# A hybrid decoder trunk on one core: VectorE, ScalarE and TensorE tied to the source's order up to the first up projection

## The chip, the core and the metric

The kernel runs on one core of a Trainium2 chip. A core has TensorE (PE in the rows of the profile, with PEld for its weight loads), VectorE (DVE), ScalarE (ACT), GpSimd (POOL) and SyncE (SP), each with a queue of instructions of its own, and DMA queues that bring data from HBM. The metric is the device time of one execution in microseconds (us).

## The reference

256 tokens of width 2048 go through two layers. Layer 0 mixes by sliding-window attention with grouped heads, layer 1 by a gated linear recurrence (HGRN2); each is followed by a squared-ReLU MLP of width 8192. Shift, scale and gate of every half layer come from a conditioning vector `c`.

```python
cond = jax.nn.silu(c)
for i in range(DEPTH):
    mod = cond @ mod_w[i] + mod_b[i]
    sh1, sc1, g1, sh2, sc2, g2 = jnp.split(mod, N_MOD, axis=-1)
    h = modulate(rms_norm(x, norm_mix[i]), sh1, sc1)
    ...
    x = x + g1[:, None, :] * y
    h = modulate(rms_norm(x, norm_mlp[i]), sh2, sc2)
    x = x + g2[:, None, :] * squared_relu_mlp(h, mlp_w1[i], mlp_w2[i])
```

In the attention `q` and `k` (32 query heads of 64, 4 key heads) are RMS-normed by head, the logits get a distance penalty (ALiBi) and a window of 128 keys, and the softmax has one more term, a learned sink per head.

## The kernel before

**Tiling.** Activations are kept transposed, 16 blocks of 128 features by 256 tokens (`x0` to `x3` hold four blocks each). Products are formed in fp32r with two parts: an operand `h` or `o` holds a high part (256 columns) and a low part (256 columns). A weight tile `raw` of 128 x 2048 comes by one DMA of 1 MB into one of 5 buffers; `prep_one` (L220) makes of each half `wh` (cast on ACT, L237) and `wl` (difference on DVE, L238). `three` (L353) issues the three matmuls of a step over a block: `wh` by the high part, `wh` by the low part, `wl` by the high part. 16 blocks, so 48 matmuls, use up one weight tile.

**What is prepared.** `prep_one` walks a list `seq` in which three kinds stand: weights; modulation rows that DVE multiplies with `cond` and sums (L226, tile `mods`); and modulation rows by a matrix-vector product on PE (`gemv`, L245): 16 matmuls `mm<-raw`, ACT's copy of the row `w<-mm` (L254), four transposes `gt` on PE, DVE's sum into `mods` (L260). `ahead` keeps it one or two weights ahead of the matmuls. `norm_first` (L468) and `norm_rstd` (L488) make the RMS norm, with a chain of small operations on `nsm`; `make_h` (L530) builds one block of the modulated input: `ht` on DVE (L534), the high part on ACT (L538), the low part on DVE (L539).

**Stages.** QKV runs over the first half of the blocks, then over two quarters, each time for ten columns (in a quarter one weight tile holds two). Within the last quarter `evac_k` (L642) and `evac_q` (L674) take a column up: a sum on DVE, a square on ACT, the matmuls `ssq` and `sst`, a chain for the reciprocal root (`head_rstd`, L617). From its third weight on, `step` (L780) is called three times behind each weight, and then until 16 steps are done. A step n issues the background queue (`hook`, L311), the product of probabilities and values of pair n-4 (`pair_v`, L751: matmuls `pv`, eight instructions in the trace, ACT's cast and DVE's low part of `o`), the transposes of pair n-3 (`pair_t`, L740: per head three transposes into the one buffer `pt`, ACT's copy `PT`), pair n itself (`pair`, L693) and up to two items of `seq` that are no weights. `pair` takes two heads: `S0` and `S1` on PE; scaling with the penalty and maximum on DVE (L707, L710); the maximum with the sink (L717 to L719); the exponentials with their sums on ACT (L720, L724); sum and reciprocal on DVE (L727, L728); and the probabilities, scaled half on ACT (L733), half on DVE (L736). Then come the out-projection and `open_mlp` (L837): residual columns between eight half products of the raw `x` (`mm_uhalf`, whose column sums go to `sums`, L877), the blocks h8 to h15 (L884 to L888), and eight rounds over the second half of the blocks (L890 to L904), in each of which a column is evacuated (L900, then the squared ReLU), one weight is read and one more block is built. The rest of the MLP and layer 1 follow.

**What sets the order.** The kernel is written once in source order; a scheduler then orders each engine's queue by the dependences, and may move an instruction ahead of others on its engine. Class `Queue` (L40) wraps an engine; where `pin` is set, each instruction gets a dependence without a semaphore on the one that this wrapper's list `last` holds, so that it can't be moved ahead of it. Before, `pep` is such a wrapper (the transposes and attention products), `pe` shares its list but isn't pinned, and DVE and ACT are used bare:

```python
dve, act, sp, pool_q = nc.vector, nc.scalar, nc.sync, nc.gpsimd
last = []
pe, pep = Queue(tc, nc.tensor, last, False), Queue(tc, nc.tensor, last, True)
```

Of the kernel before, what the change touches and what calls it, by code (L numbers as in the profile page):

```python
# [39 lines left out]
class Queue:  # L40


    def __init__(self, tc, engine, last, pin):
        self.tc, self.engine, self.last, self.pin = tc, engine, last, pin

    def __getattr__(self, name):
        fn = getattr(self.engine, name)

        def call(*args, **kw):
            r = fn(*args, **kw)  # L50
            if self.pin and self.last:
                self.tc.add_manual_dep(
                    r.ins, self.last[-1],
                    mybir.DependencyInfo(mybir.DependencyClass.NoSync, mybir.DependencyReason.DATA),
                    reason="issue order")
            self.last[:] = [r.ins.name]
            return r
        return call
# [2 lines left out]
@with_exitstack  # L61
def trunk(ctx, tc, a, out):
    nc = tc.nc
    dve, act, sp, pool_q = nc.vector, nc.scalar, nc.sync, nc.gpsimd
    last = []
    pe, pep = Queue(tc, nc.tensor, last, False), Queue(tc, nc.tensor, last, True)

# [198 lines left out]
    def prep_mods(l, which, upto=KB):  # L266
        while any((l, which * 16 + k) not in ready for k in range(upto)):
            if any(e[0] == "m" and e[1:] == (l, which * 16 + k) or e[0] == "g" and e[1] == l
                   and 0 <= which * 16 + k - e[2] < 4
                   for k in range(upto) for e in seq[st["prep"]:]):  # L270
                prep_one()
            else:
                hook()
# [32 lines left out]
    def later(delay, fn):  # L306
        bg.append((bgst["slot"] + delay, bgst["n"], fn))
        bgst["n"] += 1
        bg.sort(key=lambda e: (e[0], e[1]))
# [169 lines left out]
    def norm_add(kb):  # L479
        if kb == 0:  # L480
            nstate["ss"] = tmp.tile([P, T], F32, tag="rbs", name="ssum", bufs=1)
            act.activation(out=nstate["ss"], in_=X[kb], func=AF.Square)
            return
        sq = wt()
        act.activation(out=sq, in_=X[kb], func=AF.Square)
        dve.tensor_tensor(out=nstate["ss"], in0=nstate["ss"], in1=sq, op=ALU.add)

    def norm_rstd(sumcol=ones[:, :1]):  # L488
        ss = psum.tile([P, 2], F32, tag="sm", name="sst", bufs=1)
        for b in range(2):  # L490
            pe.matmul(ss[:, b:b + 1], lhsT=nstate["ss"][:, b * P:(b + 1) * P], rhs=sumcol,
                      start=True, stop=True)
        sm = tmp.tile([P, 8], F32, tag="nsm", name="nsm")
        dve.tensor_scalar(out=sm[:, 0:2], in0=ss, scalar1=1.0 / D, scalar2=EPS,
                          op0=ALU.mult, op1=ALU.add)
        rsqrt(sm[:, 0:2], sm[:, 2:4], sm[:, 4:6], sm[:, 6:8])
        dg = tmp.tile([P, T], F32, tag="dg", name="dg", bufs=1)
        for b in range(2):
            dve.tensor_scalar(out=dg[:, b * P:(b + 1) * P], in0=ident, scalar1=sm[:, 2 + b:3 + b],
                              scalar2=None, op0=ALU.mult)  # L500
        nstate["dg"] = dg

    def norm_bcast():
        rb = psum.tile([P, T], F32, tag="sm", name="rb", bufs=1)
        pe.matmul(rb, lhsT=ones, rhs=nstate["dg"], start=True, stop=True)
        rbs = tmp.tile([P, T], F32, tag="rbs", name="rbs", bufs=1)
        act.copy(out=rbs, in_=rb)
        return rbs
# [12 lines left out]
    def mod_prep(l, half, k0=0, n=KB):  # L521
        sh, sc = (SH1, SC1) if half == 0 else (SH2, SC2)
        mod_bias(l, sh, k0, n)
        mod_bias(l, sc, k0, n)
        g = l * 2 + half
        dve.scalar_tensor_tensor(out=gsc[:, g, k0:k0 + n],
                                 in0=mods[:, l, sc * 16 + k0: sc * 16 + k0 + n], scalar=1.0,
                                 in1=gains[:, g, k0:k0 + n], op0=ALU.add, op1=ALU.mult)

    def make_h(l, half, rbs, kb, s):  # L530
        sh = SH1 if half == 0 else SH2
        g = l * 2 + half
        t = tmp.tile([P, T], F32, tag="ht", name="ht", bufs=2)
        dve.scalar_tensor_tensor(out=t, in0=X[kb], scalar=gsc[:, g, kb:kb + 1], in1=rbs,  # L534
                                 op0=ALU.mult, op1=ALU.mult)
        shc = mods[:, l, sh * 16 + kb: sh * 16 + kb + 1]
        h = optile(sets[s], kb)
        act.activation(out=h[:, :T], in_=t, func=AF.Identity, bias=shc)  # L538
        dve.scalar_tensor_tensor(out=h[:, T:2 * T], in0=t, scalar=shc, in1=h[:, :T].bitcast(F32),  # L539
                                 op0=ALU.add, op1=ALU.subtract)  # L540
        return h
# [15 lines left out]
    def start_u(l, half, n=KB):  # L557
        sh = SH1 if half == 0 else SH2
        c = mods[:, l, sh * 16: sh * 16 + n]
        sw = tmp.tile([P, KB, 2], F32R, tag="sw", name="swt", bufs=1)  # L560
        act.copy(out=sw[:, :n, 0], in_=c)
        dve.tensor_tensor(out=sw[:, :n, 1], in0=c, in1=sw[:, :n, 0].bitcast(F32), op=ALU.subtract)
        ustate["sw"] = sw
        ustate["next"], ustate["lim"] = (l, half), n
        ustate["U"] = [None] * KB
# [5 lines left out]
    def evac_res(l, which, n):  # L571
        def f(ps):
            resid(l, which, n, ps)
            finish_x(n)
        return f
# [3 lines left out]
    def finish_x(n):  # L579
        if ustate["next"] is not None and n < ustate["lim"]:  # L580
            ustate["U"][n] = make_u(*ustate["next"], n)
        if n < KB - 1:
            later(2, lambda: norm_add(n))
        elif ustate["next"] is None:
            norm_add(n)
# [251 lines left out]
    def open_mlp(mp, A, relu2):  # L837
        prep_mods(0, SC2, KH)
        prep_mods(0, SH2, KH)
        mod_prep(0, 1, 0, KH)  # L840
        start_u(0, 1, KH)
        U = ustate["U"]
        for n in range(2):
            finish_x(n)
        parts, H, box = [], [None] * KB, {}
        sums = mp.tile([P, KB], F32, tag="sums", name="sums")

        def more_h(k0, k1):
            for k in range(k0, k1):
                H[k] = make_h(0, 1, box["rbs"], k, 0)  # L850

        def s2():
            box["rbs"] = norm_bcast()

        def s1():
            norm_rstd()
            later(NB, s2)

        def s0():
            norm_add(KB - 1)  # L860
            later(1, s1)

        def res(n):
            mm_std(O, evac_res(0, G1, n), fold=True)
            if n == KB - 1:
                later(1, s0)

        for kind, n in order[2:]:
            if kind == "o":
                res(n)  # L870
                continue
            part = mp.tile([P, 2 * T], F32, tag=f"acc{n}", name=f"part{n}")
            parts.append(part)

            def keep(u, ps):
                c = 2 * n + u
                dve.tensor_reduce(out=sums[:, c:c + 1], in_=ps[:, T:T + 2], axis=AX.X, op=ALU.add)  # L877
                act.copy(out=part[:, u * T:(u + 1) * T], in_=ps[:, :T])
            mm_uhalf(U, keep)
        while "rbs" not in box:  # L880
            hook()
        ustate["next"], ustate["lim"] = None, KB
        sets.reverse()
        for k in range(KH, KB, 2):  # L884
            prep_mods(0, SC2, k + 2)
            prep_mods(0, SH2, k + 2)
            mod_prep(0, 1, k, 2)
            more_h(k, k + 2)  # L888
        ahead(LAG - 1)
        for p in range(8):  # L890
            t2 = wt(2 * T)
            dve.tensor_tensor(out=t2.rearrange("p (a b) -> p a b", b=T),
                              in0=parts[p].rearrange("p (a b) -> p a b", b=T),
                              in1=box["rbs"].unsqueeze(1).to_broadcast([P, 2, T]), op=ALU.mult)

            def ev(ps):
                for u in range(2):
                    t = t2[:, u * T:(u + 1) * T]
                    n = 2 * p + u
                    dve.scalar_tensor_tensor(out=t, in0=ps[:, u * T:(u + 1) * T], scalar=sums[:, n:n + 1],  # L900
                                             in1=t, op0=ALU.add, op1=ALU.add)
                    relu2(A, n, t)
            mm_half(H, 1, ev)
            more_h(p, p + 1)  # L904
        return H

    def mlp_layer(l, H, last):
# [399 lines left out]
```

## Time and profile before

| what | value |
|---|---|
| runs | 2334.56, 2332.07, 2333.48 us |
| median | 2333.48 us |
| profiled execution | 2334.28 us |
| its span | 2332.5 us (1.8 us lie around it) |
| granted TensorE clock, mean | 0.987 |

A row of the profile's groups reads: line, engine, operation, out<-in (shapes), count, then busy time, mean in ns of one, and idle time before them with what ended it. A row of the timeline: start, duration, engine, line, operation, out<-in, count, and in brackets the idle time before it and its releaser. The windows give busy time and count of instructions of each engine in a stretch, the granted clock (PEclk, 1 is full), the DMA engines' busy share and GB/s.

### The profile page before, as it was taken

How to read it: one execution, taken by the hardware profiler on the slowest of the kernel's cores; microseconds unless marked ns; L12 is line 12 of the kernel's file. 1: busy time of each engine (PE TensorE's matmuls, PEld its weight loads, DVE VectorE, ACT ScalarE, POOL GpSimd, SP SyncE). 2: the span in 40 equal slices, each digit the busy share in tenths (PEclk: the TensorE clock that was granted, in tenths of full speed). 3: DMA queues.
4: the chain of work that ended last, by engine and by line, in shares of the span. 5: the costliest groups of instructions: out<-in, count | busy, mean ns of one | idle time of the engine just before them, and what ended most of it. 6: DMA issues, size and time to landing. Idle time of an engine off the chain costs nothing.

```text
span 2332.5 us, 36840 instructions
## 1 busy us (share of the span) xinstructions
PE 2263.7 (97%) x14538; PEld 1986.2 (85%) x14538; DVE 1818.7 (78%) x3061; ACT 1166.8 (50%) x1974; POOL 3.5 (0%) x10
## 2 busy tenths in 40 slices
PE   2989999999999999999999999999999999999999
PEld 0986489998888888888888988899888888888888
DVE  8888788966988988887998988767866766655665
ACT  2435754544444444455666666655544444444443
POOL 0000000000000000000000000000000000000000
PEclk6999999999999999999999999999999999999999
DMA  9987789556989889885577777545666666555552
GB/s 379 344 311 287 295 319 365 200 183 244 341 319 340 319 326 334 322 304 181 210 280 267 257 271 266 201 166 181 226 244 219 249 231 229 209 182 194 184 197 93
DMA packets 84637, 598.79 MB, mean 257 GB/s; under 512 B 9456, under 2 KB 11504, under 8 KB 12272
## 3 DMA queue, kind: packets, MB, share of 16 engines
q1 hardware_dynamic: 81936, 593.81, 70.7%
q8 instruction: 114, 1.87, 0.3%
q10 hardware_dynamic: 2304, 2.10, 0.3%
q0 software_dynamic: 224, 0.52, 0.1%
q14 instruction: 59, 0.48, 0.1%
HBM read 594.04 MB, written 2.10 MB: 256 GB/s over the span
## 4 chain that ended last, share of the span: by engine, by line
PE 94%; DVE 4%; DMA 1%; ACT 1%; issue 1%; ACTq 0%; DVEq 0%
PE mm L50 89%; DVE raw L226 2%; DVE wl L238 1%; PE S L50 1%; PE A L50 1%; PE pv L50 1%; PE pt L50 1%; DMA raw<-in_mod_w_dram 1%; PE on L50 0%; PE cb L50 0%; ACT wh L237 0%; PE ss L50 0%; DVE ht L534 0%; PE ssq L50 0%; PE sst L50 0%
## 5 line engine op out<-in xcount | busy, mean ns | idle before, releaser
L237 ACT CAST wh<-raw 128x1024 fp32r<-128x1024 f32 x744 | 779.3, 1051 | 892.3 <-PE mm L50 801.8
L238 DVE TENSOR_TENSOR wl<-raw,wh 128x1024 fp32r<-128x1024 f32 x744 | 907.3, 1223 | 401.7 <-ACT wh L237 399.3
L50 PE MATMUL mm<-h,wh 128*128 128x512 f32 (+2 forms) x3728 | 1152.6, 368 | 37.3 <-ACT wh L237 37.3
L50 PE MATMUL mm<-h,wl 128*128 128x256 f32 (+1 forms) x3232 | 907.2, 281 | 7.5 <-DVE wl L238 7.5
L50 PE MATMUL mm<-o,wh 128*128 128x512 f32 (+2 forms) x3120 | 859.1, 345 | 0.0
L50 PEld LDWEIGHTS mm<-h,wh 128*128 128x128 f32 x3728 | 672.2, 190 | 162.0 <-ACT wh L237 38.3
L50 PE MATMUL mm<-o,wl 128*128 128x256 f32 (+1 forms) x2432 | 679.5, 280 | 0.0
L50 PEld LDWEIGHTS mm<-h,wl 128*128 128x128 f32 x3232 | 612.4, 190 | 9.5 <-DVE wl L238 8.4
L50 PEld LDWEIGHTS mm<-o,wh 128*128 128x128 f32 x3120 | 538.3, 188 | 81.5 <-issue 1.3
L50 PEld LDWEIGHTS mm<-o,wl 128*128 128x128 f32 x2432 | 458.3, 189 | 0.4
L226 DVE CUSTOM_DVE_ANT_0 raw<-raw,cond 128x2048 f32<-128x2048 f32 x164 | 374.4, 2286 | 15.6 <-DMA raw<-in_mod_w_dram 11.5
L50 PE MATMUL mm<-wh,h 128*128 128x256 f32 x576 | 106.5, 284 | 4.2 <-DVE h L539 2.7
L50 PEld LDWEIGHTS mm<-wh,h 128*128 128x128 f32 x576 | 89.8, 190 | 5.3 <-DVE h L539 3.2
L50 PE MATMUL mm<-wl,h 128*128 128x256 f32 x288 | 81.5, 283 | 0.0
L459 ACT COPY w<-mm 128x256 f32<-128x256 f32 x186 | 67.7, 364 | 0.0
L463 ACT CAST h<-w 128x256 fp32r<-128x256 f32 x125 | 49.9, 404 | 25.6 <-DVE w L919 25.0
L50 PEld LDWEIGHTS mm<-wl,h 128*128 128x128 f32 x288 | 54.7, 190 | 0.6 <-issue 0.4
L919 DVE SCALAR_TENSOR_TENSOR w<-w 128x256 f32<-128x256 f32 x125 | 52.1, 423 | 2.2
L464 DVE TENSOR_TENSOR h<-w,h 128x256 fp32r<-128x256 f32 x125 | 51.7, 419 | 0.0
L460 DVE TENSOR_TENSOR w<-mm,w 128x256 f32<-128x256 f32 x109 | 45.6, 418 | 0.4 <-ACT w L459 0.2
L940 DVE TENSOR_TENSOR acc<-mm,acc 128x256 f32<-128x256 f32 x96 | 40.6, 423 | 6.2 <-PE mm L50 3.7
L939 DVE TENSOR_TENSOR acc<-acc,w 128x256 f32<-128x256 f32 x94 | 39.4, 419 | 7.1 <-ACT w L938 7.0
(200 smaller groups left out, 1098.4 us busy)
## 6 DMA issues: line engine op xcount, KB each, us to landing
raw<-in_mod_w_dram SPq DMA_DIRECT2D x164, 1024.0 KB, 5.7
raw<-in_mlp_dram SPq DMA_DIRECT2D x128, 1024.0 KB, 4.9
raw<-in_hin_dram SPq DMA_DIRECT2D x64, 1024.0 KB, 4.9
raw<-in_mlp1b_dram SPq DMA_DIRECT2D x64, 1024.0 KB, 4.9
raw<-in_mlp1a_dram SPq DMA_DIRECT2D x48, 1024.0 KB, 5.8
raw<-in_mod_g_dram SPq DMA_DIRECT2D x28, 1024.0 KB, 6.6
raw<-in_aout_dram SPq DMA_DIRECT2D x16, 1024.0 KB, 7.0
raw<-in_m1h_dram SPq DMA_DIRECT2D x16, 1024.0 KB, 6.6
```

The source lines that it names most:

```text
L50: r = fn(*args, **kw)
L226: dve.tensor_tensor_reduce(out=r, in0=r, in1=cond, scale=1.0, scalar=0.0, op0=ALU.mult, op1=ALU.add, accum_out=mods[:, e[1], e[2]:e[2] + 1])
L237: act.copy(out=wh, in_=part)
L238: dve.tensor_tensor(out=wl, in0=part, in1=wh.bitcast(F32), op=ALU.subtract)
L459: act.copy(out=t, in_=ps[:, T:])
L460: dve.tensor_tensor(out=out_t, in0=ps[:, :T], in1=t, op=ALU.add)
L463: act.copy(out=opt[:, :T], in_=src_t)
L464: dve.tensor_tensor(out=opt[:, T:2 * T], in0=src_t, in1=opt[:, :T].bitcast(F32), op=ALU.subtract)
L919: dve.scalar_tensor_tensor(out=t, in0=t, scalar=0.0, in1=t, op0=ALU.max, op1=ALU.mult)
L939: dve.tensor_tensor(out=acc[n], in0=acc[n], in1=t, op=ALU.add)
L940: dve.tensor_tensor(out=acc[n], in0=ps[:, :T], in1=acc[n], op=ALU.add)
```

## The change

`Queue` gets a switch `strict`, which is on from the start of `trunk`. DVE and ACT are wrapped as well. As long as the switch is on, each instruction of DVE, ACT and PE is tied to the one issued ahead of it on the same engine in the source, so the three queues have the source's order. At the end of `open_mlp` the switch goes off. POOL and SP stay as they are, and so does the work itself.

```diff
 class Queue:
+    strict = True
...
-            if self.pin and self.last:
+            if (self.pin or Queue.strict) and self.last:
...
-    dve, act, sp, pool_q = nc.vector, nc.scalar, nc.sync, nc.gpsimd
+    sp, pool_q = nc.sync, nc.gpsimd
+    Queue.strict = True
+    dve, act = Queue(tc, nc.vector, [], False), Queue(tc, nc.scalar, [], False)
...
             mm_half(H, 1, ev)
             more_h(p, p + 1)
+        Queue.strict = False
         return H
```

In the rows of the changed kernel, the wrapped engines' instructions carry the wrapper's line, L52, instead of their own.

**The first place is DVE in attention**, around one pair of heads (tiles `h6` and `h7` hold its logits, then its probabilities; `asm_2552` its small numbers, `asm_2490` those of the pair before it). Before:

```order
L707 SCALAR_TENSOR_TENSOR h6_2553<-S0_2549,qw_1966,dist_343 128x128
L707 SCALAR_TENSOR_TENSOR h7_2554<-S0_2549,qw_1966,dist_343 128x128
L710 TENSOR_REDUCE asm_2552<-h6_2553 128x1
L710 TENSOR_REDUCE asm_2552<-h7_2554 128x1
L707 SCALAR_TENSOR_TENSOR h6_2553<-S1_2548,qw_1966,dist_343 128x256
L707 SCALAR_TENSOR_TENSOR h7_2554<-S1_2548,qw_1966,dist_343 128x256
L727 TENSOR_TENSOR asm_2490<-asm_2490 128x4
L710 TENSOR_REDUCE asm_2552<-h6_2553 128x1
L728 RECIPROCAL asm_2490<-asm_2490 128x4
L710 TENSOR_REDUCE asm_2552<-h7_2554 128x1
L736 TENSOR_SCALAR h4_2491<-h4_2491,asm_2490 128x256
L736 TENSOR_SCALAR h5_2492<-h5_2492,asm_2490 128x256
```

And in the changed kernel, on the same engine, from the second reduction of the pair's second head to the first scaling of the next pair (`h8`):

```order
L52 TENSOR_REDUCE asm_2552<-h7_2554 128x1
L52 TENSOR_TENSOR asm_2552<-asm_2552,cst_70 128x4 x3
L52 TENSOR_TENSOR asm_2552<-asm_2552 128x4
L52 RECIPROCAL asm_2552<-asm_2552 128x4
L52 TENSOR_SCALAR h6_2553<-h6_2553,asm_2552 128x256
L52 TENSOR_SCALAR h7_2554<-h7_2554,asm_2552 128x256
L52 TENSOR_REDUCE mods_81<-gt_2589 128x4
L52 TENSOR_TENSOR o8_2602<-pv_2597,o8_2602 128x256
L52 SCALAR_TENSOR_TENSOR h8_2622<-S0_2618,qw_2169,dist_343 128x128
```

The sum and the reciprocal of a pair, which need ACT's exponentials, stood behind the next pair's scalings; now they stand ahead of them, directly behind the pair's own maxima.

**The second place is PE in the same step**: the transposes `pt` of an earlier pair, the modulation product `mm<-raw`, and the next pair's `S0` and `S1`. Before:

```order
L50 MATMUL pt_2605<-cst_70,h2_2422 128x128 x3
L50 MATMUL mm_2646<-raw_2464,cst_70 32x512
L50 MATMUL pt_2611<-cst_70,h3_2423 128x128 x3
L50 MATMUL S0_2618<-kz3_348,o14_895 128x256
L50 MATMUL S1_2617<-kz3_348,o14_895 128x512
L50 MATMUL mm_2646<-raw_2464,cst_70 32x512 x3
```

In the changed kernel:

```order
L52 MATMUL pt_2605<-cst_70,h2_2422 128x128 x3
L52 MATMUL pt_2611<-cst_70,h3_2423 128x128 x3
L52 MATMUL S0_2618<-kz3_348,o14_895 128x256
L52 MATMUL S1_2617<-kz3_348,o14_895 128x512
L52 MATMUL mm_2646<-raw_2464,cst_70 32x512 x4
```

The two groups of transposes, which share one buffer, stand back to back, and all of the modulation product comes behind `S1`.

**The third place is DVE ahead of the up projection's second half**, where the blocks `o8` to `o15` are built (`ht` and then the low part) between the last sums of the products of `x` (`sums`) and the weights' low parts (`wl`). Before:

```order
L534 SCALAR_TENSOR_TENSOR ht_4592<-x2_75,gsc_139,rbs_4471 128x256
L534 SCALAR_TENSOR_TENSOR ht_4597<-x2_75,gsc_139,rbs_4471 128x256
L892 TENSOR_TENSOR w_4641<-part0_3704,rbs_4471 128x512
L877 TENSOR_REDUCE sums_3086<-mm_4456 128x1
L539 SCALAR_TENSOR_TENSOR o8_4594<-ht_4592,mods_81,o8_4594 128x256
L539 SCALAR_TENSOR_TENSOR o9_4599<-ht_4597,mods_81,o9_4599 128x256
```

In the changed kernel:

```order
L52 TENSOR_REDUCE sums_3086<-mm_4552 128x1
L52 TENSOR_TENSOR wl_4580<-raw_4238,wh_4579 128x1024
L52 TENSOR_TENSOR wl_4584<-raw_4238,wh_4583 128x1024
L52 TENSOR_TENSOR mods_81<-mods_81,cst_70 128x2 x2
L52 SCALAR_TENSOR_TENSOR gsc_139<-mods_81,cst_70 128x2
L52 SCALAR_TENSOR_TENSOR ht_4592<-x2_75,gsc_139,rbs_4471 128x256
L52 SCALAR_TENSOR_TENSOR o8_4594<-ht_4592,mods_81,o8_4594 128x256
L52 SCALAR_TENSOR_TENSOR ht_4597<-x2_75,gsc_139,rbs_4471 128x256
L52 SCALAR_TENSOR_TENSOR o9_4599<-ht_4597,mods_81,o9_4599 128x256
```

Four of the sixteen sums (`mm_4456` to `mm_4552`, the last) stood behind the first `ht`; now all stand ahead of it, and the blocks follow one at a time.

## The prediction

> **What bounds the kernel now.** I read the totals first, then busy time by stage, then the groups, the timeline and the chain of waits of the stages that the change touches. The page's totals and its chain:
>
> ```profile
> span 2332.5 us, 36840 instructions
> PE 2263.7 (97%) x14538; PEld 1986.2 (85%) x14538; DVE 1818.7 (78%) x3061; ACT 1166.8 (50%) x1974; POOL 3.5 (0%) x10
> PE 94%; DVE 4%; DMA 1%; ACT 1%; issue 1%; ACTq 0%; DVEq 0%
> ```
>
> PE is the bound, with 69 us of idle time in all. Busy time by stage (start of the span to the first weight; QKV without and with its last quarter; attention; out-projection and residual; h8 to h15 and the first half of the up projection; the rest):
>
> ```profile
> core 0: us, PE busy (x) PEld busy (x) DVE busy (x) ACT busy (x) POOL busy (x), PEclk, DMA share, GB/s
> 0.00:62.80 62.80, 14.38 (x46) 5.61 (x46) 52.89 (x111) 14.91 (x35) 0.87 (x5) 0.67 0.97 377
> 62.80:166.40 103.60, 96.14 (x744) 95.13 (x745) 89.30 (x104) 42.19 (x52) 0.00 (x0) 0.92 0.89 333
> 166.40:190.45 24.05, 23.84 (x182) 17.97 (x180) 19.49 (x64) 10.99 (x18) 2.07 (x4) 1.00 0.60 193
> 190.45:308.05 117.60, 114.48 (x737) 63.93 (x737) 87.70 (x356) 75.91 (x248) 0.00 (x0) 1.00 0.79 304
> 308.05:425.00 116.95, 116.95 (x987) 116.90 (x986) 103.99 (x154) 56.73 (x88) 0.00 (x0) 1.00 0.92 339
> 425.00:481.00 56.00, 56.00 (x470) 55.61 (x469) 55.32 (x109) 33.97 (x54) 0.00 (x0) 1.00 0.52 177
> 481.00:2332.50 1851.50, 1841.89 (x11382) 1631.07 (x11380) 1409.98 (x2169) 932.12 (x1481) 0.57 (x1) 1.00 0.68 243
> ```
>
> What the reader is to see: from 190 us on PE is full, and DVE is 75% full in attention and 99% in the stage up to 481. That fullness rests on interleaving: while a pair of heads waits for ACT, DVE works on the next pair and PE on weights. The tie removes this freedom on all three engines. It adds and removes no instruction. POOL's and SP's orders stay, so the DMAs are issued in the same order, only later. From 481 us on the order on every engine is the one of before; that stage, 1851.5 us, I cost at nothing: its loads come later by as much as all else, and DMA is at 0.68 of its time there. If a load were late at the seam all the same, one weight tile of 1.05 MB at 243 GB/s is 4.3 us. The sum therefore concerns 481 us.
>
> **Start, +8.5.** The rows of DVE and ACT:
>
> ```profile
> 12.77 2.29 DVE L226 CUSTOM_DVE_ANT_0 raw<-raw,cond 128x2048 f32<-128x2048 f32 x1 [4.16 <-ACT cond L112]
> 19.64 0.16 DVE L494 TENSOR_SCALAR nsm<-sst 128x2 f32<-128x2 f32 x1 [2.36 <-PE sst L50]
> 20.23 0.16 DVE L135 TENSOR_TENSOR nsm<-nsm 128x2 f32<-128x2 f32 x1
> 20.43 0.16 DVE L136 SCALAR_TENSOR_TENSOR nsm<-nsm 128x2 f32<-128x2 f32 x1
> 57.59 0.88 DVE L534 SCALAR_TENSOR_TENSOR ht<-x,gsc,rbs 128x256 f32<-128x256 f32 x2
> 60.91 0.91 ACT L538 ACTIVATE h<-ht,mods 128x256 fp32r<-128x256 f32 x2 [10.23 <-DVE mods L518]
> 61.45 0.89 DVE L539 SCALAR_TENSOR_TENSOR h<-ht,mods,h 128x256 fp32r<-128x256 f32 x2 [0.57 <-ACT h L538]
> ```
>
> Before, two reductions of modulation rows (the first at 12.77, 2.2 us each) ran while DVE waited for `sst`. Tied, the whole `nsm` chain, eleven dependent small operations, stands ahead of them, so 2 x 2.2 = 4.4 us move into a stretch where DVE sets the end. Second, the four groups of two `h` are built one by one: `ht` on DVE, ACT's `h`, the low part on DVE. A single `h` in order takes about 1.43 us (0.45 + 0.5 + 0.45 and handover) against 0.8 when two overlap; a pair then costs 2.86 against 1.59, +1.27 for three groups and +0.7 for the last. 4.4 + 3.8 + 0.7 is 8.9; some of it lies beside what DVE waits for anyway, so 8.5, with 8 and 9 as the ends.
>
> **QKV up to its last quarter, +1.8.** PE's busy time of 96.1 in 103.6 leaves little; DVE builds h12 to h15 there, four times +0.63 at most (2.4), 1 at least.
>
> **Last quarter, +8 and 3 us owed.** The head norms have a chain like `nsm`, 13 small operations, most of them 0.2 us apart (20.23 and 20.43), 2.15 us in all. PE now meets each `ssq` and `sst` in the source's place, where the DVE sum, ACT's square or that chain is not done, instead of running weight matmuls first. Walking the order by those durations, PE stalls 0.3 + 1.5 + 2.05 + 2.35 + 3.2 + 3.7 = 13.1 us, while twelve matmuls of the modulation product `mm<-raw`, 3.0 us before, come only behind the first `S`, and 2.1 of small matmuls now lie inside the stalls: 24.05 - 3.0 - 2.1 + 13.1 = 32.0 us to the first `S`, with 3.0 still to do. Together +11 on the way to the out-projection.
>
> **Attention, +87 on top of those 11.** Sixteen pairs of heads. The groups of this window, and one pair's waits in the timeline:
>
> ```profile
> L707 DVE SCALAR_TENSOR_TENSOR h<-S,qw,dist 128x256 f32<-128x256 f32 x32 | 14.7, 476 | 0.5 <-PE S L50 0.4
> L707 DVE SCALAR_TENSOR_TENSOR h<-S,qw,dist 128x128 f32<-128x128 f32 x32 | 10.2, 346 | 11.8 <-PE S L50 11.8
> L710 DVE TENSOR_REDUCE asm<-h 128x1 f32<-128x256 f32 x32 | 12.7, 407 | 0.0
> L710 DVE TENSOR_REDUCE asm<-h 128x1 f32<-128x128 f32 x32 | 8.1, 277 | 0.0
> L747 ACT COPY PT<-pt 128x384 f32<-128x384 f32 x32 | 15.1, 473 | 9.7 <-PE pt L50 8.5
> L254 ACT COPY w<-mm 128x512 f32<-128x512 f32 x7 | 4.1, 580 | 5.2 <-PE mm L50 5.2
> 276.82 0.21 ACT L720 ACTIVATE asm<-asm 128x4 f32<-128x4 f32 x1 [0.29 <-DVE asm L719]
> 278.59 0.19 ACT L724 ACTIVATION_READ_ACCUMULATOR h<-h,asm 128x1 f32 x1
> 279.31 0.70 ACT L733 ACTIVATE h<-h,asm 128x128 f32<-128x128 f32 x2
> 279.46 0.55 PE L50 MATMUL pt<-cst,h 128*128 128x128 f32 x3 [0.91 <-ACT PT L747]
> 279.84 1.46 PE L50 MATMUL S<-kz,o 128*128 128x256 f32 x4
> 280.48 0.61 DVE L707 SCALAR_TENSOR_TENSOR h<-S,qw,dist 128x128 f32<-128x128 f32 x2 [0.46 <-PE S L50]
> ```
>
> In the source's order a pair is one ring. DVE: two heads, each two scales and two reductions that need one another, 2 x (0.35 + 0.28 + 0.48 + 0.41) = 3.0, 3.3 with handovers. Three small operations, 0.6. ACT: from 276.82 to the last accumulator, 278.78, 2.0. DVE's sum and reciprocal, 0.5 up to 279.31, and ACT's two scalings there (0.70): 7.1 us after the ring's start. Nothing else of DVE or ACT stands in between. The next step's `pv` and first `pt` need PE only, but ACT's cast of `o` and copy of the first `PT` (0.47) queue behind the scalings: 7.7. `pt` has one buffer, so PE's second `pt` waits for that copy, three transposes take 0.4 (279.46 to 279.84), then `S`, and 0.64 later (279.84 to 280.48) DVE begins the next ring: **8.8 us**. Where a row copy `w<-mm` (0.58) stands in the step, PE's `gt` transposes, eight `pv` and the first `pt` (some 1.8) queue behind a copy that itself queues behind the scalings: **11.15 us**. The chain of waits shows what the last nine rounds cost before:
>
> ```profile
> 233.65 1.29 PE S L50 x4
> 285.53 1.29 PE S L50 x4
> ```
>
> 51.9 us. Tied: five at 8.8 and four at 11.15 are 88.6. The first six rounds took 43.1 (190.5 to 233.65); tied they are, by the order, 9.1 and 6.9 without transposes (DVE's own 6.9, up to its two scalings beside ACT's, one with a norm chain of 2.2), 11.0 and 11.15, two that hold a quarter of the weights, each 7.1 for the pair, 5.7 for 48 matmuls and waits of 3.7 and 4.4 at `ssq`, 20.9, and three reductions of 2.2 that DVE takes in line: 9.1 + 6.9 + 11.0 + 11.15 + 2 x 20.9 + 6.6 = 86.6. Behind the last pair: 22.5 before; now the last ring's 7.1 and four casts of 1.05 stand ahead of the weights, of which I let 0.8 overlap: 33. The sum 86.6 + 88.6 + 33 = 208.2 against 117.6 is +90.6; less the 3 owed, counted above, +87.
>
> **Out-projection and residual, +4.4.** The first two weights wait 0.8 more; DVE's cycle per weight with the residual becomes 6.35 against PE's 5.68 (48 matmuls of 116.95/987) over a few weights, +2.9, and the norm behind it +0.65.
>
> **h8 to h15 and the first half, +35.5.** DVE is at 55.3 of 56.0 there, so each in-order wait is paid.
>
> ```profile
> 434.46 0.15 DVE L877 TENSOR_REDUCE sums<-mm 128x1 f32<-128x2 f32 x1
> 62.78 2.36 DVE L238 TENSOR_TENSOR wl<-raw,wh 128x1024 fp32r<-128x1024 f32 x2 [0.45 <-ACT wh L237]
> 440.48 0.87 DVE L900 SCALAR_TENSOR_TENSOR w<-mm,sums,w 128x256 f32<-128x256 f32 x2
> 441.71 0.74 ACT L463 CAST h<-w 128x256 fp32r<-128x256 f32 x2 [0.27 <-DVE w L919]
> ```
>
> Before, `ht` and its partners ran from 424 us between the eight sums, while PE still had columns to do. Tied, all eight `h` stand behind the last sum (434.46 before) and two `wl` (2.36): 2.36 + 8 x 1.43 + 3.6 for twelve small scale operations and handovers is 17.4 us in which PE has little: +15. Then come eight rounds, one weight each. Seven of them cost DVE about 8.6: two evacuations with ACT's cast between their operations, 2 x 1.76, `wl` 2.3, an `h` 1.43, and the rest 1.4, while PE needs 5.68: 7 x 2.9 = 20.5.
>
> **The clock, +20 (5 to 35).** Three idle times of PE in QKV, and a window behind one:
>
> ```profile
> 137.91 0.58 PE L50 MATMUL mm<-h,wl 128*128 128x256 f32 x1 [2.76 <-DVE wl L238]
> 146.73 0.38 PE L50 MATMUL mm<-h,wl 128*128 128x256 f32 x1 [1.29 <-DVE wl L238]
> 155.63 0.58 PE L50 MATMUL mm<-h,wl 128*128 128x256 f32 x1 [2.94 <-DVE wl L238]
> 138.00:140.00 2.00, 2.00 (x9) 2.00 (x10) 2.00 (x4) 1.66 (x2) 0.00 (x0) 0.50 0.67 254
> ```
>
> After 2.76 and 2.94 us the clock fell to 0.50 and a matmul took 0.58 instead of 0.38; after 1.29 us nothing. At half clock for some 3 us, PE loses up to 2. Tied, idle times of 3 us and more follow about ten times: 10 x 2. If every bare round loses it too, 35; if hidden behind ACT, 5.
>
> [...]
>
> **Sum:** 8.5 + 1.8 + 11 + 87 + 4.4 + 35.5 + 20 = 168. The profiled execution took 2334.28 (span 2332.5 and 1.8 around it), so 2502; the median of the runs, 2333.48, lies 0.8 below it, so 2501 or 2502. I take **2502**.
>
> **Rivals.**
> *Only DVE's own round counts* (0.14). ACT and PE keep up: bare and `gt` rounds both cost 6.9, DVE's ring without the next step's copies. The nine rounds give 62 instead of 88.6, the first six about 10 less, the up projection 10 less, and no clock is lost: 2502 - 27 - 10 - 10 - 17 = **2438**. For it: PE's `pt` waited only 0.91 at 279.46. Against it: one buffer of `pt`.
> *Half clock throughout attention* (0.14). [...]
> *Not slower* (0.03). PE's waits for `wl` in the second quarter, 2.76 + 1.29 + 2.94 = 7.0, and about 3.7 of clock behind them are 10.7 us that an earlier `wl` would save, if the source puts it ahead of DVE's other work; with the start's 8.5 this gives **2332**, provided a tied pair costs under (10.7 - 8.5)/16 = 0.14 us more. The ring of 8.8 against 5.8 speaks against it.
> *The tie does nothing* (0.01): the orders differ in most rows up to 481 us.
>
> **Chances and range.** The forecast 0.66, the rivals as above, 0.02 for more than the second. Low end 2428 (the first rival less 10), high end 2555 (the second and 10), which leaves out about 0.15. A measurement of this kernel tells about 0.2%, 4.7 us: faster 0.01, same 0.02, slower 0.97.
>
> **What would show it.** Right: in attention `S` starts 8 to 11 us apart and DVE and PE both well under full; the stage from 190 us some 90 longer; DVE's `ht` behind the last `sums`, with PE idle over 10 us there; granted clock below 1 after such gaps; the end stage at 1851 us. Wrong: `S` under 7 apart, or a first up projection at PE's 5.7 per weight; or losses behind the last tied row, through DMAs that start late.

## The result, and the profile after

The changed kernel takes 2517.15 us (median of four runs, 2513.85 to 2517.36) against 2334.02 of before (four runs): 1.0783 times the time, 95% interval 1.0764 to 1.0801. That is +183 us; the forecast was 2502 with 2428 to 2555, +168. The profiled execution of the changed kernel is its fastest, 2513.85 us; its span is 2512.1, 179.6 more than before's. All comparisons of stages below are made between spans.

The page's totals and the chain of the changed kernel:

```profile
span 2512.1 us, 36840 instructions
PE 2316.1 (92%) x14538; PEld 2011.8 (80%) x14538; DVE 1844.5 (73%) x3061; ACT 1166.8 (46%) x1974; POOL 3.5 (0%) x10
PE 81%; DVE 12%; ACT 4%; issue 2%; DMA 1%; ACTq 0%; DVEq 0%
```

The same instructions, and 13 points less of the chain on PE: DVE and ACT have taken them. PE's busy time grew by 52 us though no matmul was added: the same matmuls took longer (the 128x512 `S` of attention 884 ns on average, 595 before), at a granted clock of 0.72 and 0.77 in attention, where it was 1.00 before. Busy time by stage of the changed kernel (about the last quarter of QKV; attention's first six rounds and last nine; to the out-projection's third column; to the last `sums`; to the end of the tied part; the rest):

```profile
core 0: us, PE busy (x) PEld busy (x) DVE busy (x) ACT busy (x) POOL busy (x), PEclk, DMA share, GB/s
...
176.00:211.76 35.76, 24.94 (x169) 20.34 (x167) 18.63 (x67) 10.96 (x19) 2.06 (x4) 0.86 0.30 104
211.76:304.58 92.82, 55.63 (x275) 29.29 (x273) 45.94 (x159) 26.18 (x88) 0.00 (x0) 0.72 0.40 147
304.58:406.05 101.47, 62.19 (x301) 27.66 (x301) 47.53 (x163) 36.64 (x130) 0.00 (x0) 0.77 0.45 166
406.05:446.45 40.40, 29.62 (x189) 20.23 (x189) 14.97 (x31) 15.54 (x31) 0.00 (x0) 0.83 0.33 114
446.45:575.14 128.69, 127.28 (x1062) 126.21 (x1061) 104.66 (x147) 56.77 (x91) 0.00 (x0) 1.00 0.87 325
575.14:660.60 85.46, 66.30 (x405) 59.09 (x406) 58.09 (x113) 29.24 (x47) 0.00 (x0) 0.82 0.31 109
660.60:2512.10 1851.50, 1842.45 (x11368) 1630.97 (x11366) 1412.73 (x2172) 934.94 (x1484) 0.57 (x1) 1.00 0.69 243
```

The last boundary lies as far from the end as before's, 1851.5 us; PE's instructions behind it are 11368, 11382 before. The reader is to see three things. In attention no engine is busy for more than 62% of the time, and DMA, which was at 0.79 there, is at 0.40 to 0.45: every engine waits for another. The clock is 0.72 to 0.86 in the five stages in which PE idles much. And the stage from 446 to 575, where PE stays full, takes nearly what it took before (126.4 there).

Of the attention, four groups whose waits grew (line, engine, operation, shapes, count; busy us and mean ns; idle time before them and its releaser):

```profile
L52 PE MATMUL pt<-cst,h 128*128 128x128 f32 x78 | 18.8, 365 | 26.6 <-ACT PT L52 26.6
L52 PE MATMUL gt<-cst,w 128*128 128x128 f32 x24 | 6.7, 434 | 33.4 <-ACT w L52 33.4
L52 ACT ACTIVATE asm<-asm 128x4 f32<-128x4 f32 x15 | 3.1, 206 | 71.7 <-DVE asm L52 71.7
L52 DVE SCALAR_TENSOR_TENSOR h<-S,qw,dist 128x128 f32<-128x128 f32 x30 | 10.4, 346 | 19.2 <-PE S L52 19.1
```

PE waits for ACT's copies (`PT`, the row `w`), ACT for DVE's maxima, DVE for PE's `S`: these are the legs of the ring. One round of it in the timeline, from one `S` to the next:

```profile
360.82 1.46 PE L52 MATMUL S<-kz,o 128*128 128x256 f32 x4
361.45 0.35 DVE L52 SCALAR_TENSOR_TENSOR h<-S,qw,dist 128x128 f32<-128x128 f32 x1 [1.00 <-PE S L52]
...
365.30 0.21 ACT L52 ACTIVATE asm<-asm 128x4 f32<-128x4 f32 x1 [3.80 <-DVE asm L52]
...
367.76 0.69 ACT L52 ACTIVATE h<-h,asm 128x128 f32<-128x128 f32 x2 [0.50 <-DVE asm L52]
368.36 0.56 ACT L52 COPY w<-mm 128x512 f32<-128x512 f32 x1
368.97 1.11 PE L52 MATMUL gt<-cst,w 128*128 128x128 f32 x4 [4.84 <-ACT w L52]
370.02 1.55 PE L52 MATMUL pv<-PT,vnat 128*64 128x256 f32 x8
371.50 0.90 PE L52 MATMUL pt<-cst,h 128*128 128x128 f32 x3
372.44 0.48 ACT L52 COPY PT<-pt 128x384 f32<-128x384 f32 x1 [0.45 <-PE pt L52]
372.97 0.55 PE L52 MATMUL pt<-cst,h 128*128 128x128 f32 x3 [0.57 <-ACT PT L52]
373.36 1.03 PE L52 MATMUL S<-kz,o 128*128 128x256 f32 x3
```

This is a round with a row copy: 373.36 - 360.82 = 12.54 us, and every step stands where the order puts it. ACT is through with the scalings 7.0 us after DVE began (368.45 against 361.45); then come row copy, `gt`, `pv`, `pt`, copy, `pt`, `S`, one behind the other. A bare round skips from the scalings to the copy of `PT`; the shortest took 8.7.

The end of the tied part, DVE's row by row:

```profile
575.14 0.16 DVE L52 TENSOR_REDUCE sums<-mm 128x1 f32<-128x2 f32 x1 [1.82 <-PE mm L52]
576.68 2.36 DVE L52 TENSOR_TENSOR wl<-raw,wh 128x1024 fp32r<-128x1024 f32 x2 [1.38 <-ACT wh L52]
...
579.42 0.49 DVE L52 SCALAR_TENSOR_TENSOR ht<-x,gsc,rbs 128x256 f32<-128x256 f32 x1
580.48 0.48 DVE L52 SCALAR_TENSOR_TENSOR o<-ht,mods,o 128x256 fp32r<-128x256 f32 x1 [0.58 <-ACT o L52]
580.88 0.48 DVE L52 SCALAR_TENSOR_TENSOR ht<-x,gsc,rbs 128x256 f32<-128x256 f32 x1
...
592.06 0.48 DVE L52 SCALAR_TENSOR_TENSOR o<-ht,mods,o 128x256 fp32r<-128x256 f32 x1 [0.58 <-ACT o L52]
...
598.21 0.49 DVE L52 SCALAR_TENSOR_TENSOR w<-mm,sums,w 128x256 f32<-128x256 f32 x1 [5.06 <-PE mm L52]
...
606.86 0.48 DVE L52 SCALAR_TENSOR_TENSOR w<-mm,sums,w 128x256 f32<-128x256 f32 x1
```

A block costs 1.46 us (579.42 to 580.88), the eight are done 17.3 us after the last sum, and a round of the up projection takes 8.65 (598.21 to 606.86).

Where the 179.6 us lie, by landmarks that both traces have, beside what the prediction's terms without the clock give for the same stretch:

| stretch | before | after | difference | worked out |
|---|---|---|---|---|
| start to the first weight | 62.80 | 72.56 | +9.8 | +8.5 |
| first weight to first `S` | 127.65 | 139.20 | +11.6 | +9.8 |
| first six rounds of attention | 43.0 | 92.8 | +49.8 | +43.5 |
| last nine rounds | 51.9 | 101.5 | +49.6 | +36.7 |
| last `S` to the out-projection's third column | 22.7 | 40.4 | +17.7 | +10.3 |
| from there to the last `sums` | 126.4 | 128.7 | +2.3 | +4.4 |
| from the last `sums` to the end | 1898.0 | 1937.0 | +38.9 | +35.5 |

### The profile page after: what moved, and what is told of

It reads as the page before. It is cut to its first block, busy times and chain, and to the rows that moved or that the text cites. A ratio compares the mean times of both kernels' runs of the same rounds, so it can differ in the third digit from the quotient of the medians.

```text
span 2512.1 us, 36840 instructions
## 1 busy us (share of the span) xinstructions
PE 2316.1 (92%) x14538; PEld 2011.8 (80%) x14538; DVE 1844.5 (73%) x3061; ACT 1166.8 (46%) x1974; POOL 3.5 (0%) x10
## 4 chain that ended last, share of the span: by engine, by line
PE 81%; DVE 12%; ACT 4%; issue 2%; DMA 1%; ACTq 0%; DVEq 0%
PE mm L52 76%; DVE raw L52 3%; DVE wl L52 3%; ACT h L52 2%; DVE asm L52 1%; DVE h L52 1%; PE S L52 1%; ACT wh L52 1%; DVE w L52 1%; DMA raw<-in_mod_w_dram 1%; PE pt L52 1%; DVE o L52 1%; PE A L52 1%; DVE qw L52 1%; DVE ht L52 1%
## 5 line engine op out<-in xcount | busy, mean ns | idle before, releaser
L52 PE MATMUL mm<-h,wh 128*128 128x512 f32 (+2 forms) x3728 | 1157.6, 369 | 55.9 <-ACT wh L52 51.0
L52 DVE TENSOR_TENSOR wl<-raw,wh 128x1024 fp32r<-128x1024 f32 x744 | 904.0, 1223 | 403.6 <-ACT wh L52 401.5
L52 ACT CAST wh<-raw 128x1024 fp32r<-128x1024 f32 x744 | 775.0, 1050 | 842.3 <-PE mm L52 749.2
L52 PE MATMUL mm<-h,wl 128*128 128x256 f32 (+1 forms) x3232 | 908.9, 282 | 6.4 <-DVE wl L52 6.4
L52 PE MATMUL mm<-o,wh 128*128 128x512 f32 (+2 forms) x3120 | 872.5, 349 | 19.5 <-ACT wh L52 11.0
L52 PEld LDWEIGHTS mm<-h,wh 128*128 128x128 f32 x3728 | 674.8, 191 | 183.5 <-ACT wh L52 57.1
L52 PE MATMUL mm<-o,wl 128*128 128x256 f32 (+1 forms) x2432 | 685.3, 282 | 6.2 <-DVE wl L52 6.2
L52 PEld LDWEIGHTS mm<-o,wh 128*128 128x128 f32 x3120 | 546.2, 191 | 105.9 <-ACT wh L52 13.9
L52 PEld LDWEIGHTS mm<-h,wl 128*128 128x128 f32 x3232 | 614.6, 190 | 8.3 <-DVE wl L52 8.0
L52 PEld LDWEIGHTS mm<-o,wl 128*128 128x128 f32 x2432 | 462.9, 190 | 8.8 <-DVE wl L52 8.4
L52 DVE CUSTOM_DVE_ANT_0 raw<-raw,cond 128x2048 f32<-128x2048 f32 x164 | 373.6, 2285 | 10.9 <-DMA raw<-in_mod_w_dram 10.9
L52 PE MATMUL mm<-wh,h 128*128 128x256 f32 x576 | 108.3, 287 | 2.8 <-DVE h L52 2.2
L52 ACT COPY w<-mm 128x256 f32<-128x256 f32 (+1 forms) x287 | 106.0, 369 | 7.1 <-PE mm L52 7.1
L52 PEld LDWEIGHTS mm<-wh,h 128*128 128x128 f32 x576 | 91.3, 193 | 4.3 <-DVE h L52 2.9
L52 PE MATMUL mm<-wl,h 128*128 128x256 f32 x288 | 82.1, 285 | 0.0
L52 ACT CAST h<-w 128x256 fp32r<-128x256 f32 x125 | 50.5, 404 | 53.9 <-DVE w L52 53.3
L52 DVE TENSOR_TENSOR h<-w,h 128x256 fp32r<-128x256 f32 x125 | 52.4, 419 | 7.6 <-ACT h L52 7.6
L52 PEld LDWEIGHTS mm<-wl,h 128*128 128x128 f32 x288 | 55.6, 193 | 0.3
L52 DVE SCALAR_TENSOR_TENSOR w<-w 128x256 f32<-128x256 f32 x125 | 52.9, 423 | 2.8
L52 PE MATMUL pt<-cst,h 128*128 128x128 f32 x96 | 22.1, 351 | 28.4 <-ACT PT L52 28.4
L52 DVE SCALAR_TENSOR_TENSOR h<-S,qw,dist 128x128 f32<-128x128 f32 x64 | 26.4, 412 | 29.8 <-PE S L52 29.6
L52 ACT ACTIVATE h<-ht,mods 128x256 fp32r<-128x256 f32 x32 | 15.4, 504 | 65.9 <-DVE ht L52 65.9
```

## The experiments

Each kernel below was run once, except the rewritten step without ties. The changed kernel's own four runs lie 3.5 us apart, so a difference of that size between two kernels is not clear of noise.

### One tie at a time

Each of three kernels keeps the tie on one engine. The wrapper gets one more field (here for DVE; `pe` gets it too):

```diff
-            if (self.pin or Queue.strict) and self.last:
+            if (self.pin or Queue.strict and self.tie) and self.last:
...
-    dve, act = Queue(tc, nc.vector, [], False), Queue(tc, nc.scalar, [], False)
+    dve, act = Queue(tc, nc.vector, [], False, True), Queue(tc, nc.scalar, [], False, False)
```

> Only DVE keeps the tie; ACT and PE are ordered by the scheduler as before. Theory of the rings (the loss is a round of waits through DVE, ACT and PE, each engine's order holding one leg of it): DVE alone keeps the start (+9), a round of 6.9 to 7.5 us a pair in attention instead of 5.8 (+20 to +30 there, not +99), and most of the first up projection (h8 to h15 still behind the last sum, +15, and some of the 8.6 a round): 2390 to 2420 us. Rival (DVE's order alone carries the loss): 2490 or more. Rival (only the three ties together cost, one alone is mended by the other two queues): under 2350.

> Only ACT keeps the tie. Theory of the rings: ACT's copy of PT stays behind a pair's exponentials and scalings, and the one pt buffer makes PE's S wait for it, so that the attention keeps rounds of 8 to 9 us (the last nine 75 to 85 us instead of 52, the first six about 60 instead of 43), while the start and the up projection lose under 10 together: 2390 to 2420 us. Rival (DVE carries the loss): under 2350. Rival (only the three together cost): under 2350.

> Only PE keeps the tie. Theory of the rings: PE waits at ssq and sst in the source's place (+8 to +15 in and behind the last quarter of QKV and at the quarters inside attention), and the modulation product no longer fills the waits between the two transposes, +0 to +1 a pair: 2345 to 2365 us. Rival (PE's own order is the loss, because nothing fills its waits): 2420 or more. Rival (DVE carries it): within 0.5% of before.

Measured: DVE alone 2455.62 us, ACT alone 2423.45, PE alone 2364.2 (before, on the same chip, 2334.22): +121, +89 and +30. The three sum to 240, more than the +183 of all together, so the parts overlap. By stages of the spans:

| tie on | first `S` | first six | last nine | last `S` to last `sums` | last `sums` to end |
|---|---|---|---|---|---|
| none (before) | 190.5 | 43.0 | 51.9 | 149.1 | 1898.0 |
| DVE | 206.2 | 76.9 | 62.9 | 166.4 | 1941.6 |
| ACT | 191.0 | 70.8 | 92.1 | 161.9 | 1906.0 |
| PE | 194.5 | 52.4 | 62.0 | 154.6 | 1898.9 |
| all (after) | 211.8 | 92.8 | 101.5 | 169.1 | 1937.0 |

The column of the last nine rounds decides. ACT alone brings them to 92.1, with rounds of 7.9 to 8.9 and 12.5 to 13.3 us in turn: nearly the whole ring. DVE alone makes the last six rounds 6.6 to 7.3 each. A round of the kernel with ACT tied, DVE free:

```profile
290.37 1.46 PE L52 MATMUL S<-kz,o 128*128 128x256 f32 x4
...
296.51 0.69 ACT L52 ACTIVATE h<-h,asm 128x128 f32<-128x128 f32 x2 [0.50 <-DVE asm L52]
297.11 0.56 ACT L52 COPY w<-mm 128x512 f32<-128x512 f32 x1
...
297.73 1.11 PE L52 MATMUL gt<-cst,w 128*128 128x128 f32 x4 [5.91 <-ACT w L52]
...
302.90 1.46 PE L52 MATMUL S<-kz,o 128*128 128x256 f32 x4
```

It is the leg through ACT's queue, scalings before copies, that sets the round, as worked out; DVE's own round is only a second, shorter bound. The start and the up projection belong to DVE: +43.6 behind the last `sums` with DVE tied, +8.0 with ACT, +0.9 with PE. The expectation for DVE alone was too low by 36 us: the first six rounds with their quarters of weights (+34) and the way to the first `S` (+16) cost more than I had put down, and the way from the last `S` to the last `sums` (+17) I hadn't put down at all. That for ACT missed by 3 us at the upper end, and its rounds by more: 92.1 in the last nine where 75 to 85 were expected, 70.8 in the first six where it was about 60. PE's held.

### The switch off ahead of the blocks h8 to h15

```diff
         ustate["next"], ustate["lim"] = None, KB
         sets.reverse()
+        Queue.strict = False
         for k in range(KH, KB, 2):
```

> All three ties, but the switch goes off ahead of the blocks h8 to h15 instead of behind the up projection. If the +38.9 us between the last sum and the end of the tied part are the waits of that part's order alone, they go: 2478 us (2472 to 2486). If part of it is carried in from attention (DMAs that came late, weights not ready), only the part goes that the order makes: 2490 or more. If what follows also pays, under 2470.

Measured 2474.47 us, span 2472.7. Behind the last `sums` it takes 1898.4, before's 1898.0: the 38.9 us there were that part's own order, all of them, and nothing was carried in from attention.

### The row of `gt` two hooks later

```diff
                 ready.update((l, col + j) for j in range(4))
-            fin()
+            later(2, fin)
```

> All three ties; the transposes of a modulation row and DVE's sum of them are put two hooks later in the source, so that PE no longer waits at gt for ACT's row copy behind a pair's scalings. If the extra 3.7 us of a round with gt (13.4 against 9.6) are that wait, the four in the last nine rounds fall to 9.5 to 10.5 us each, and two or three in the first six as well: 18 to 26 us in all, 2491 to 2499 us. If PE would have waited for the copy of PT behind the same scalings anyway, it gives 0 to 5 us: 2512 or more.

Measured 2492.84 us, span 2491.0: -21.1. The last nine rounds take 88.3 us, those with a row copy 9.5 to 10.5 in place of 12.5 to 13.9; the first six 85.5. So the wait behind the row copy is worth some 3.4 us a round (13.4 to 10).

### Matmuls that keep PE busy

Each step issues three matmuls that nothing uses; `S1` overwrites them.

```diff
+        def warm(n):
+            spare[n] = psum.tile([P, 2, T], F32, tag="sA", name="S1", bufs=2)
+            for _ in range(3):
+                pep.matmul(spare[n], lhsT=ident, rhs=xt[0][:, :2, :], start=True, stop=True)
...
             hook()
+            if s_ < 16:
+                warm(s_)
```

> All three ties; each step issues three more matmuls of 128x512 into S1 ahead of pv, whose result S1 overwrites. They do no work that is used; they fill PE's wait after the second head's maximum. If part of the loss is the lower clock behind idle times over 2.8 us (attention's last nine rounds 13 us and the first six 6 us above the rounds that I worked out), the granted clock in attention goes from 0.72 to 0.77 to over 0.9, rounds go from 9.6 and 13.4 to 8.8 and 11.3, and the time falls by 12 to 22 us: 2495 to 2505. If the rounds are long by their waits alone, the added 2.6 us a step are hidden or come on top: 2515 to 2545.

Measured 2526.85 us, span 2525.1: +13.0, which lies in the range of the rival, that the rounds are long by their waits alone. But the granted clock of the last nine rounds rose from 0.77 to 0.92 (over the whole span from 0.955 to 0.966), and bare rounds all fell to 8.71; those with `gt` rose to 15.3, since there the three stood behind `gt`, on the way to `pv`. The run mixes two effects and decides little by itself. So the same with `gt` out of the way, against the kernel with `gt` later alone:

> All three ties, gt two hooks later, and the three matmuls a step that S1 overwrites. Nothing of gt waits behind them any more (with gt in its old place they stood on the way, 15.3 us a round). If the clock is what was left of a round, the clock in the last nine rounds goes to over 0.95, bare rounds take 8.7 us, those with a row copy 8.7 + 0.6 = 9.3, the nine together 79 to 83 instead of 88.3, and the time is 2478 to 2488 us against 2492.8 without them. If these matmuls only cost, over 2493.

Measured 2491.07 us, 1.8 less than without them, outside the expectation; but the place that it was about did what was expected. The last nine rounds take 80.6 in place of 88.3, bare ones 8.71 and those with a row copy 9.2, five and four of them, at full clock where it was 0.84 without the added matmuls (the nine rounds in that kernel; over the whole span 0.971 and 0.963):

```profile
305.19:385.77 80.58, 68.94 (x356) 30.26 (x355) 46.83 (x163) 35.82 (x130) 0.00 (x0) 1.00 0.56 209
```

The 7.7 us won there are the price of the clock in that kernel's last nine rounds. They are given back before: the first `S` comes 5.6 us later (216.5 against 210.9), of which 4.7 are the first step's added matmuls (a row of 4.91 us, where the second step's takes 2.84), and the first six rounds take 3.2 more. Behind the last `S` another 2.8 are won.

### The blocks h two at a time

```diff
-                for j in range(2):
-                    self.H.append(make_h(l, half, rbs, self.k + j, 0))
+                self.H += make_hs(l, half, rbs, [self.k, self.k + 1], 0)
```

Here `make_hs` issues both `ht`, both high parts, both low parts; the blocks h8 to h15 of the up projection are built by it as well.

> All three ties; the blocks h are issued two at a time in the source (two ht, two high parts, two low parts), everywhere but in the up projection's rounds. If a block costs 1.45 us in order because DVE waits for ACT between its two operations, a pair falls from 2.9 to 1.6 or 1.7: the first weight comes 4.5 to 5 us earlier (67.5 to 68 instead of 72.6), h12 to h15 give 1 to 2.5 and h8 to h15 of the up projection another 4.5 to 5, in all 9 to 12.5 us: 2505 to 2508. If the start hangs on loads of modulation rows instead, the first weight stays over 71 and the time over 2510.

Measured 2501.26 us, under the expected range, which was reckoned from the changed kernel's median; its profiled run lies 3 us below that median, and by spans it is 2499.5 against 2512.1, -12.6. The first weight comes at 68.15 (-4.4), the first `S` 8.4 earlier, so that the stretch with h12 to h15 gave 4.0, more than the 2.5 allowed; behind the last `sums` 4.6 are won. The wait of DVE for ACT inside one block (0.58 us in the changed kernel's rows) is what the in-order block costs.

### The step rewritten, with the ties kept

The same operations, in a source that is pipelined by hand: `S` of the next pair behind this pair's exponentials, a pair's sum, reciprocal and scalings one step later, the low part of `o` behind them, and `gt` later as above.

```diff
+            if n > 0:
+                rest.pop(n - 1)()
+            low()
             act.activation(out=es, in_=es, func=AF.Exp)
...
-            dve.tensor_tensor(out=l, in0=l, in1=es, op=ALU.add)
...
+            if n + 1 in qts:
+                score(n + 1)
+
+            def scale():
+                dve.tensor_tensor(out=l, in0=l, in1=es, op=ALU.add)
...
+            rest[n] = scale
```

> All three ties; the source of a step is rewritten with the same operations: S of the next pair is issued behind this pair's exponentials, a pair's sum, reciprocal and scalings come one step later, between the next pair's maxima and its exponentials, the low part of o comes behind them, and gt two hooks later. If the loss in attention is the round that the source's order makes, and not the tie as such, no leg is left that goes through all three engines: DVE needs 5.3 us, ACT about 4.5, PE 6 a pair, so that the last nine rounds take 55 to 66 us instead of 101 and the first six 65 to 80 instead of 93: 2440 to 2465 us. If the tie as such costs (each engine idle at every handover, late loads, clock), rounds stay over 8 us: over 2490.

Measured 2444.69 us, span 2442.9: -69.2. From the first `S` to the last it takes 126.4 in place of 194.3; `S` now stands a step ahead, so that one quarter of the weights falls in the last nine gaps (70.3) and one in the first six (56.0), which puts both outside what was expected of them. The time is inside, and the five last rounds take 5.8, 6.5, 5.6, 6.2 and 5.8 us, before's mean of 5.8 (51.9 by nine) at last. In these rounds the tie as such costs next to nothing; the order that it enforces did.

Without the ties the rewritten step is to show whether it frees anything that bound the kernel before:

> The rewritten step, without any tie beyond the old one on PE's transposes and attention products. If PE was full in attention before, the scheduler has nothing to gain from the rewritten source: within 0.3% of before, 2328 to 2341 us. If the rewriting frees something that also bound the kernel before, under 2326.

Measured 2334.26 us (ten runs) against 2333.68 (thirteen): 1.0002, interval 0.9993 to 1.0012. Where PE was full already (114.5 of attention's 117.6 us before), the rewriting wins nothing.

### The tie in attention alone, and all rewrites together

> The three ties hold from the first step of attention to the sixteenth and nowhere else. If the loss there is made by the order of the steps themselves, the first S comes at 190 to 192 us as before, the first six rounds take 86 to 93 us, the last nine 99 to 102, the way from the last S to the last sum is within 6 us of before's 149, and what follows takes before's 1898: 2425 to 2440 us, 60% of the whole loss. If attention's rounds are long because weights and rows arrive late from the tied start (the last nine under 85), under 2415.

In this kernel the switch goes on at the first step and off behind the sixteenth. Measured 2422.2 us, 3 under the expected range. The first six rounds take 92.5 and the last nine 102.0, those of the fully tied kernel (92.8 and 101.5), so their length owes nothing to what lies ahead of them. The first `S` came at 187.1 and the way from the last `S` to the last `sums` took 140.4, 8.7 under before's: with the queues free around it, the scheduler moved work into attention's waits (675 matmuls between the first `S` and the last, 569 before).

> All three ties up to h8, with three rewrites of the source together: the pipelined step with gt later, the blocks h in pairs, and the switch off ahead of h8. If the parts of the loss lie one behind the other in the program, the gains add up: spans of 69.2 (pipelined step) + 39.4 (off ahead of h8) + 8.1 (pairs up to the last sum) off 2512.1 give 2395 us of span, 2390 to 2402 us of time. If they share one cause (the clock, late loads), the sum of the gains is smaller than that: over 2408.

Measured 2395.7 us, span 2393.9: the three gains add up to within 1.5 us. What is left, 61.4 us of span, is the start and QKV (first `S` at 202.8, +12.4), attention (123.2 between first and last `S`, +28.3) and the way to the last `sums` (169.6, +20.5). No version with ties was faster than the kernel before.

## Why the prediction was right

- **That the change costs, and where.** Right: the rings, `ht` behind the last `sums`, and the end stage at before's time were all where the prediction put them. Three of its signs came out in kind but not in size: rounds with a row copy went over 11 us, the stage from the first `S` to the out-projection's third column grew by 117 us and not some 90, and PE idled 7.7 us, not over 10, in the 17.3 behind the last `sums`. That the end stage is as it was is shown by the kernel with the switch off ahead of h8: 1898.4 us behind the last `sums`, 1898.0 before.
- **The bare round, 8.8.** 8.71 at full clock (with the added matmuls), 8.7 to 10.3 in the changed kernel. That it closes through ACT's queue is shown by the tie on ACT alone.
- **The round with a row copy, 11.15.** 12.5 to 13.9. The clock makes the difference plausible: in the round shown, `gt`, `pv` and `pt` take 1.05, 1.48 and 0.94 us to the next instruction (ACT's copy behind `pt`), where full clock took 0.59 (before, from 275.64), 0.80 and 0.58 (changed kernel, from 356.21 and 360.44): together 1.5 more, and 12.54 - 1.5 is 11.0.
- **The start, +8.5**, was +9.8: 4.4 of it are the blocks one by one, as the blocks two at a time show; the reductions of modulation rows weren't tried apart. **h8 to h15, 17.4 us**, were 17.3; **a round of the up projection, 8.6**, was 8.65.
- **The first rival**, DVE's own round of 6.9, is what the tie on DVE alone shows (6.6 to 7.3); it didn't hold here because ACT was tied too. **The second**, half clock throughout, is half of the truth: 0.72 and 0.77 in attention. No run shows that rival's time, ten under the range's high end of 2555; with those clocks the changed kernel took 2517.15.
- **The clock, +20, was worked out wrongly.** The table's differences beyond the other terms sum to 31 us, of which 12.9 lie in the last nine rounds, 6.2 in the first six and 7.4 behind them; that attention's part, 19, is near 20 is luck. The step that was wrong is "at half clock for some 3 us, PE loses up to 2", ten times. Behind the first idle time that it names, of 2.76 us, it is so: windows of 0.2 us show 0.50 from 137.7 to 141.1. Behind the one of 2.94 us they show 0.50 from 154.7 to 161.5, 6.8 us, though PE works without a gap from 155.63 on. In the changed kernel's attention the clock falls fourteen times, and is at 0.50 for 3.4 us five times, 6.8 five times, 10.2 three times and 17 once. One fall of 10.2 us, around an idle time of 3.74 us that ended at 346.11, and one of 3.4, in the round shown above (windows of 2 us):

```profile
342.00:344.00 2.00, 0.37 (x4) 0.00 (x0) 0.34 (x3) 1.56 (x8) 0.00 (x0) 1.00 0.83 229
344.00:346.00 2.00, 0.00 (x0) 0.00 (x0) 0.96 (x4) 1.50 (x5) 0.00 (x0) 0.76 0.94 360
346.00:348.00 2.00, 1.89 (x8) 1.24 (x10) 0.17 (x1) 0.06 (x1) 0.00 (x0) 0.50 0.97 389
...
354.00:356.00 2.00, 2.00 (x16) 0.36 (x8) 1.87 (x6) 0.00 (x0) 0.00 (x0) 0.68 0.00 0
356.00:358.00 2.00, 1.56 (x15) 0.80 (x11) 0.48 (x3) 1.40 (x8) 0.00 (x0) 1.00 0.81 201
...
368.00:370.00 2.00, 1.03 (x4) 0.71 (x4) 0.31 (x2) 0.92 (x3) 0.00 (x0) 0.73 0.95 401
372.00:374.00 2.00, 1.43 (x8) 0.96 (x7) 0.43 (x2) 0.92 (x2) 0.00 (x0) 0.91 0.00 0
```

  The first of these reaches into the next round's `S`, and that bare round takes 10.0 us. Three of the five bare rounds take 10.0 to 10.3, the two others 8.7. How much of the 31 us is clock is shown only for the kernel with `gt` later, 7.7 us of its last nine rounds; for the rest it is argued from such windows. Counted from where PE begins to work without a gap, the clock is back after 3.4 us in the round shown (from 368.97), 5.2 in the one before it (from 350.11) and 5.9 in QKV (from 155.63).
- **The way behind the last `S`, +10.3, was +17.7.** The order there puts a second set of four casts, 3.9 us, ahead of the last row copy and its `gt`, which the walk had at 0.8 for both weights; the last `S`, at a clock of 0.50 from 406.05 on, takes 2.70 us to the next instruction, where full clock took 1.38 (from 360.82). This wasn't tried apart.

## What to carry to other kernels

Before tying queues to the source, walk one round of the loop through all engines: what an engine's order holds back is a leg of the round only if someone waits for it, and the longest closed round, not the sum of busy times, was the price here (8.7 to 10.3 us a bare round, 5.8 on average before). A tie cost next to nothing in the rounds whose source was already pipelined (the last five of the rewritten step), and without ties that pipelining gave nothing, since PE, the bound engine, was full. Where a change leaves TensorE idle in every round, price the clock over the whole round, not for a single restart: here it was at 0.50 for 3.4 to 17 us at a time.

## What was not expected

In these runs the clock didn't fall at one fixed idle time. In the changed kernel PE idled 2.88 us ahead of the `pt` at 360.44 and the window from 360 to 362 shows 1.00; before, 2.76 and 2.94 us brought 0.50. And a single tied queue can cost two thirds of what three cost: the scheduler, free on the other two, didn't mend the waits that DVE's order made.
